# A hybrid encoder block on one core: the half's norm and gate as a second thread, joined key norms, four gate groups beside the mixers, turned values as a thread

## Chip, cores and metric

The kernel runs on one core of a Trainium2 chip. The metric is the device time of one execution in microseconds (us). A difference within 0.5% is treated as no change. The engines are named as in the profile: PE multiplies matrices, PEld loads its weights, DVE is the vector engine, ACT the scalar (activation) engine, POOL the general one, and SP issues most of the DMAs.

## What is computed

The input `x` is 256 positions of 2048 features. One layer is computed:

```python
u = RMSNorm(x)
proj = u @ w_in        # stick-breaking q,k,v | forgetting q,k,v,f | RWKV r,k,v + low-rank | three gates
y_A = stick_breaking_attention(...)    # 4 heads of 128
y_B = forgetting_attention(...)        # 4 heads of 128
y_C = rwkv7_time_mix(...)              # 16 heads of 64
m = sum_i sigmoid(gate_i) * (y_i @ P_i)
x = x + RMSNorm(m @ w_out)
x = x + RMSNorm(relu(RMSNorm(x) @ w_up)**2 @ w_down)
```

The RWKV mixer is a recurrence over positions. Its keys are normalised per head, and its output `y` goes through a group norm per head, a bonus term and a gate:

```python
kk = kk / max(sqrt(sum(kk*kk)), 1e-12)
state = state * w_t - (state @ kk_t) * kka_t + v_t * k_t ;  y_t = state @ r_t
y = (y - mean) * rsqrt(var + eps) * ln_w + ln_b + sum(r*k*r_k) * v ;  y_C = y * g
```

All values are float32. The large products split each factor into a rounded part (type fp32r) and a remainder, and add three of the four products of these parts.

## The kernel before

**Weights and the large products.** The weights lie in memory as one list of blocks of 128x1024 values (512 KB). `wraw` loads a block into one of three `raw` buffers through the SP queue. `wsplit` makes `whi` from it on ACT (line 140) and `wlo` on DVE (line 141); `wnext` keeps one block split ahead of the one in use. Three helpers use the blocks. `unit` makes 128 output features for all 256 positions from two blocks (`gemm`, lines 156, 160 and 164). `tok` makes 512 output features with positions on the partitions; a block of it is twelve PE instructions of 512 columns (lines 187 and 203).

**The order of the work on PE** is written by hand: from the start to the end of the branches PE runs its instructions in program order (`manual_schedule`, held open by `written`). The instructions of the other engines are ordered by a list scheduler: they may go as soon as what they read is there, and earlier program order has priority. So a PE instruction whose input is late holds all of PE, and the matmuls behind it too.

**The mixers are a generator.** `mixers()` emits stick-breaking attention (`sb_mix`), forgetting attention (`fox_mix`), the low-rank parts (`rwkv_lora`) and then the two halves of the RWKV heads (`rwkv_half(0)`, `rwkv_half(1)`), a few instructions at a time. It yields either a number, the us that have to pass before its next piece, or a key, the name of a value that it needs. The products call `tick` after each few matmuls. `tick` moves a clock of the program forward by `US` = 0.227 us for each matmul it counts and calls `step`, which emits the mixers' next pieces if their time has come. A key counts as there `SETTLE` = 2.6 us after it was marked. This clock knows only the matmuls of the large products, and it is a matter of emission order: nothing on the chip waits for it.

**A half** (`rwkv_half`, four groups of two heads) goes through these stages: key norms in two pairs (lines 522 to 548, with Ln and Exp on ACT); for each group the scores, decays and bonus (552 to 615); a transposed copy of the values (617 to 627); the inverse of 32 triangular blocks in 31 steps on DVE (635 to 645) and two small products that complete it (655 to 669, PE lines 657 and 664); a loop over four chunks of 64 positions that carries the state (678 to 726, PE lines 683, 687, 696, 706, 710 and 714); and the group norm, bonus and gate in two pairs (737 to 763, PE lines 746, 759 and 760; `rsqrt` has Ln and Exp on lines 227 and 228). The small PSUM results of the mixers share four buffers (`mps`), the large products have four others (`gps`).

**After the projections** the kernel runs four groups of gate and branch for y_A and y_B, then two groups of gate for y_C (`thc`, line 867), with the mixers between them. What the mixers have left then is emitted at once by the loop of lines 868 to 870, with no product between. After it come the split of y_C into `ycp`, two branches for y_C, the two last gates, the two last branches, and between these the transposed values of m (`turn`, line 878), which w_out needs as `mpk`.

Of the kernel before, what the change touches and what calls it, by code (L numbers as in the profile page):

```python
# [17 lines left out]
T = 256  # L18
# [32 lines left out]
def hybrid_block(ctx, tc, xt, x, gains, params, consts, lora, gup, wst, out):  # L51
# [43 lines left out]
    mix = [None]  # L95
    wait = [None]
    fin = [False]
    clock, due = [0.0], [0.0]

    def step():  # L100

        if mix[0] is None or fin[0]:
            return False
        if wait[0] is not None:
            if wait[0] not in at or clock[0] < at[wait[0]] + SETTLE:
                return False
            wait[0] = None
        try:
            r = next(mix[0])
        except StopIteration:  # L110
            fin[0] = True
            return False
        if isinstance(r, str):
            wait[0] = r
        else:
            due[0] = clock[0] + r
        return True

    def tick(us):

        clock[0] += us
        while clock[0] >= due[0] and step():
            pass

# [27 lines left out]
    def gemm(ps, hi, lo, pks, first, last, tick=lambda us: None):  # L152

        n = len(pks)
        for i in range(n - 1 if last else n):
            PE.matmul(ps, hi[:, i * 128:i * 128 + 128], pks[i], start=first and i == 0, stop=False)  # L156
            if i % 3 == 2:
                tick(3 * US)
        for i in range(n):
            PE.matmul(ps[:, 0:T], lo[:, i * 128:i * 128 + 128], pks[i][:, 0:T], start=False, stop=False)  # L160
            if i == 3:
                tick(4 * US)
        if last:
            PE.matmul(ps, hi[:, (n - 1) * 128:n * 128], pks[n - 1], start=False, stop=True)  # L164
        tick(4 * US)
# [241 lines left out]
    def fox_mix():  # L407
# [17 lines left out]
        yield 10.0  # L425
# [15 lines left out]
        for h in range(4):  # L441
            ps = mps()
            PE.matmul(ps[:, 0:128], q[h][:, 0:128], k[h][:, 0:128], start=True, stop=True)
            PE.matmul(ps[:, 128:384], q[h][:, 128:256], k[h], start=True, stop=True)
            V.scalar_tensor_tensor(w[:, h, 0:128], ps[:, 0:128], ATT_SCALE, cb[:, h, 0:128], ALU.mult, ALU.subtract)
            V.scalar_tensor_tensor(w[:, h, 128:384], ps[:, 128:384], ATT_SCALE, cb[:, h, :], ALU.mult, ALU.subtract)
            V.scalar_tensor_tensor(w[:, h, 0:128], w[:, h, 0:128], ct[:, h:h + 1], C("madd"), ALU.add, ALU.add)
            V.tensor_scalar(w[:, h, 128:256], w[:, h, 128:256], ct[:, 4 + h:5 + h], None, ALU.add)
            V.scalar_tensor_tensor(w[:, h, 256:384], w[:, h, 256:384], ct[:, 4 + h:5 + h], C("madd"),
                                   ALU.add, ALU.add)  # L450
            if h % 2:
                yield 6.0
# [54 lines left out]
    def rwkv_half(hf):  # L507
# [13 lines left out]
        lora_load(PR[0])  # L521
        for i2 in range(2):
            ss = []
            for p in PR[2 * i2:2 * i2 + 2]:
                yield f"k{p}"
                kx[p] = done[f"k{p}"]
                s = tmp()
                A.activation(s, kx[p], AF.Square, scale=P("kk", p))
                ss.append(s)
            yield 2.4  # L530
            ps = mps()
            for i in range(2):
                PE.matmul(ps[:, i * T:i * T + T], C("bones"), ss[i], start=True, stop=True)

            ri = B6[:, 2 * i2:2 * i2 + 2, :]
            sc = B6[:, 4:6, :]
            sq = rp.tile([128, 2, T], F32, tag="At", name=nm("sq"), bufs=2)
            V.tensor_scalar(sq, ps.rearrange("p (a b) -> p a b", a=2), 1e-24, None, ALU.max)
            A.activation(sc, sq, AF.Ln, scale=float(2.0 ** 20))
            A.activation(ri, sc, AF.Exp, scale=-0.5)  # L540
            yield 2.5
# [3 lines left out]
            V.tensor_tensor(sc, sc, sq, ALU.mult)  # L545
# [71 lines left out]
        XT = []  # L617
        for i2 in range(2):
# [59 lines left out]
        for c in range(4):  # L678
# [13 lines left out]
            yield 2.6  # L692
# [8 lines left out]
            yield 2.8  # L701
# [24 lines left out]
            yield 3.4  # L726

        gqs = {}
# [8 lines left out]
        gup_load(PR[0])  # L737
        for i2 in range(2):
            B6 = rp.tile([128, 6, T], F32, tag="b6", name=nm("gn"), bufs=1)
            var, ri, sc = B6[:, 0:2, :], B6[:, 2:4, :], B6[:, 4:6, :]  # L740
            for i in range(2):
                A.activation(sc[:, i, :], y[PR[2 * i2 + i]], AF.Square)
            yield 2.4
            ps = mps()
            for i in range(2):
                PE.matmul(ps[:, i * T:i * T + T], C("bones"), sc[:, i, :], start=True, stop=True)
            A.activation(var, ps.rearrange("p (a b) -> p a b", a=2), AF.Identity, scale=1.0 / 64, bias=cst[:, 1:2])
            yield 1.5
            rsqrt(ri, var, sc)
            yield 6.0  # L750
            for i in range(2):
                p = PR[2 * i2 + i]
                V.tensor_tensor(y[p], y[p], ri[:, i, :], ALU.mult)
                A.activation(y[p], y[p], AF.Identity, scale=P("lnw", p), bias=P("lnb", p))
                V.tensor_tensor(y[p], y[p], bon[p], ALU.add)
                gup_load(p + 1)
                gq = gqs[p]
                ps = mps()
                PE.matmul(ps[:, 0:T], gq[:, 0, :], sy, start=True, stop=False)
                PE.matmul(ps[:, 0:T], gq[:, 1, :], sz, start=False, stop=True)  # L760
                V.tensor_tensor(y[p], ps[:, 0:T], y[p], ALU.mult)
                yc[p] = y[p]
                yield 2.5
# [8 lines left out]
    mix[0] = mixers()  # L772
# [10 lines left out]
    def mark(key, value=True):  # L783
        done[key], at[key] = value, clock[0]

    g0 = 16 + 8 + 6 + 16 + 8 + 48
    order.extend(range(wpos[0], g0))
# [3 lines left out]
    for g in (0, 2):  # L791
        for i in (0, 8):
            order.extend(c0 + 12 * (g + j) + k for j in range(2) for k in (range(8) if i == 0 else range(8, 12)))

    for br in ("sb", "fox"):
        for s in ("q", "k"):
            if br == "sb":
                continue
            lst = []
            for h in range(4):  # L800
                ps = unit(upk)
                t = g1()
                evac(ps, t)
                lst.append(t)
            done[br + s] = lst
        done[br + "v"] = vtok()
        mark(br)
        if br == "sb":
            for i, (nme, n) in enumerate((("zx", 128), ("zy", 128), ("zz", 36))):
                ps = unit(upk)  # L810
                z = rp.tile([128, T], F32, name=nme)
                if n < 128:
                    G.memset(z, 0.0)
                shift(ps, MU_X + i, z[0:n], n)
                done[nme] = z
            mark("lora")
# [11 lines left out]
    while "yb" not in done:  # L828
        assert step() or not fin[0]
    ya, yb = done["ya"], done["yb"]  # L830

    def gate(spare=False):
        ths = []
        for ps in tok(upk):
            if spare:
                th = [g1(), g1()]
            else:
                t = rp.tile([128, 512], F32, tag="th", name=nm("th"), bufs=3)
                th = [t[:, 0:T], t[:, T:]]
            if spare:  # L840
                for i in range(2):
                    A.activation(th[i], ps[:, i * T:i * T + T], AF.Tanh, scale=0.5)
            else:
                A.activation(t, ps, AF.Tanh, scale=0.5)
                th = [t]
# [3 lines left out]
    def branch(ys, ths, m, first):  # L849

        for tt, ps in enumerate(tok(ys)):
            n = 512 // len(ths[tt])
            for i, th in enumerate(ths[tt]):
                cs = slice(i * n, i * n + n)
                if first:
                    V.scalar_tensor_tensor(m[:, tt, cs], th, 1.0, ps[:, cs], ALU.add, ALU.mult)
                else:
                    V.scalar_tensor_tensor(th, th, 1.0, ps[:, cs], ALU.add, ALU.mult)
                    V.tensor_tensor(m[:, tt, cs], m[:, tt, cs], th, ALU.add)

    ms = []
    for g in range(4):
        m = rp.tile([128, 2, 512], F32, tag="m", name=nm("m"), bufs=4)
        branch(ya, gate(), m, True)
        branch(yb, gate(), m, False)
        ms.append(m)
    thc = [gate(), gate(True)]
    while not fin[0]:
        due[0] = clock[0]
        step()  # L870
# [5 lines left out]
    mpk = []  # L876

    def turn(g):

        for j in range(4):  # L880
            ps = mps()
            for tt in range(2):
                PE.transpose(ps[:, tt * 128:tt * 128 + 128], ms[g][:, tt, j * 128:j * 128 + 128], C("ident"))
            u = pk()
            split(ps[:, 0:T], u, 0.5)
            mpk.append(u)

    branch(ycp, thc[0], ms[0], False)
    branch(ycp, thc[1], ms[1], False)
    thc = [gate(), gate(True)]  # L890
    turn(0)
    branch(ycp, thc[0], ms[2], False)
    turn(1)
    branch(ycp, thc[1], ms[3], False)
    turn(2)
    turn(3)
    written.close()
# [43 lines left out]
    for g in range(4):  # L941
        gs = slice(512 * g, 512 * g + 512)
        for tt, ps in enumerate(tok(mpk, 4 if g == 3 else 1)):
# [419 lines left out]
```

## Time and profile before

| | |
|---|---|
| median of three runs | 1579.47 us (1574.84 to 1582.13) |
| the profiled execution, its own time | 1581.91 us |
| its span from first to last instruction | 1580.1 us |
| mean granted PE clock | 0.982 of full speed |
| weights and other input read | 279.77 MB |
| part looked at here | from the start to about 860 us: projections, mixers, gates, branches, w_out |

In the profile a row of the timeline gives the start, the length, the engine, the line of the kernel, the operation and its operands, and, in brackets, the idle time of the engine before it and what released it. A row of the table by stages gives, for each stretch, its length and for each engine the busy time and the number of instructions, then the granted PE clock, the share of time in which the DMA engines were busy, and their GB/s. A matmul of the mixers (plain fp32) is two PE instructions in the trace: the 32 of line 657 are 64.

### The profile page before, as it was taken

The numbers are of one execution on the slowest core, as the hardware profiler recorded it, in microseconds if no ns is written. First come the engines' busy times: TensorE is split into PE (matmuls) and PEld (weight loads), VectorE is DVE, ScalarE is ACT, GpSimd is POOL, SyncE is SP. The second block draws the span as 40 slices with busy tenths as digits, with TensorE's granted clock in tenths as the row PEclk, the third lists the DMA queues.
The fourth block names the chain that finished last, engine by engine and source line by source line (L and its number), as shares of the span: only waits on it lengthen the run. The fifth ranks groups of instructions, "written<-read, shape, count | busy, mean of one in ns | idle before, by whom it ended". The sixth has DMA issues, their size and how long they took to land.

```text
span 1580.1 us, 22365 instructions
## 1 busy us (share of the span) xinstructions
PE 1530.9 (97%) x8318; PEld 1279.6 (81%) x8318; DVE 1160.4 (73%) x1566; ACT 901.7 (57%) x1340; POOL 85.8 (5%) x155
## 2 busy tenths in 40 slices
PE   7999999999999999779999999999999999999997
PEld 6888888888788788668888788887888887888885
DVE  6875567797457789255654867888988899888855
ACT  7564467554457553254444766666765676666542
POOL 0020001100000100000000000000000000000000
PEclk9999999999999999689999999999999999999999
DMA  7645555456445545126595466878888887888764
GB/s 260 190 154 182 168 166 172 150 169 201 142 144 172 165 158 173 55 71 192 178 329 202 151 189 180 248 230 260 249 258 235 231 264 227 266 239 239 211 203 135
DMA packets 101053, 308.50 MB, mean 195 GB/s; under 512 B 10064, under 2 KB 12496, under 8 KB 100816
## 3 DMA queue, kind: packets, MB, share of 16 engines
q1 hardware_dynamic: 90624, 278.56, 53.4%
q0 software_dynamic: 6912, 25.17, 8.6%
q10 hardware_dynamic: 3408, 3.34, 0.6%
q8 instruction: 65, 1.06, 0.3%
q14 instruction: 44, 0.36, 0.1%
HBM read 279.77 MB, written 2.10 MB: 178 GB/s over the span
## 4 chain that ended last, share of the span: by engine, by line
PE 72%; issue 11%; DMA 9%; DVE 5%; ACT 2%; POOL 0%; ACTq 0%; POOLq 0%; DVEq 0%; SPq 0%
PE gps L203 29%; PE gps L156 15%; PE gps L160 8%; PE gps L187 6%; DMA raw<-raw 5%; DMA raw<-in_wst_dram 4%; DVE wlo L141 2%; ACT whi L140 1%; PE gps L164 1%; PE mps L1128 1%; PE mps L1130 1%; PE mps L1129 1%; PE gps L1130 1%; PE gps L1128 1%; PE gps L1129 1%
## 5 line engine op out<-in xcount | busy, mean ns | idle before, releaser
L141 DVE TENSOR_TENSOR wlo<-raw,whi 128x1024 fp32r<-128x1024 f32 x590 | 717.0, 1224 | 259.7 <-ACT whi L140 236.5
L140 ACT ACTIVATE whi<-raw 128x1024 fp32r<-128x1024 f32 x590 | 618.5, 1055 | 352.2 <-PE gps L203 130.5
L156 PE MATMUL gps<-pk,whi 128*128 128x512 f32 x1495 | 382.8, 394 | 1.1 <-DVE tmp L1051 1.0
L156 PEld LDWEIGHTS gps<-pk,whi 128*128 128x128 f32 x1495 | 277.3, 189 | 59.4 <-issue 5.1
L203 PE MATMUL gps<-whi,pk 128*128 128x512 f32 x1144 | 288.8, 392 | 0.0
L203 PEld LDWEIGHTS gps<-whi,pk 128*128 128x128 f32 x1144 | 213.9, 188 | 44.9 <-issue 0.5
L160 PEld LDWEIGHTS gps<-pk,wlo 128*128 128x128 f32 x1599 | 218.6, 190 | 16.0 <-issue 0.6
L160 PE MATMUL gps<-pk,wlo 128*128 128x256 f32 x1599 | 224.6, 282 | 0.0
L203 PE MATMUL gps<-wlo,pk 128*128 128x512 f32 x572 | 155.7, 392 | 0.0
L203 PEld LDWEIGHTS gps<-wlo,pk 128*128 128x128 f32 x572 | 106.9, 188 | 23.1 <-issue 0.7
L1128 PE MATMUL mps<-whi,fm 128*128 128x512 f32 x192 | 76.3, 397 | 0.8 <-ACT whi L140 0.7
L1130 PE MATMUL mps<-wlo,fm 128*128 128x512 f32 x192 | 75.8, 395 | 0.8 <-DVE wlo L141 0.8
L1050 ACT ACTIVATE tmp<-gps 128x256 f32<-128x256 f32 x64 | 24.6, 384 | 89.1 <-PE gps L164 88.8
L1129 PE MATMUL mps<-whi,fm 128*128 128x512 f32 x192 | 75.1, 391 | 0.0
L187 PE MATMUL gps<-whi,pk 128*128 128x512 f32 x264 | 71.8, 393 | 0.9 <-DVE pk L220 0.8
L1095 POOL DMA_DIRECT2D raw<-raw x48 | 41.9, 873 | 555.3 <-DVE raw L1092 360.0
L1130 PE MATMUL gps<-wlo,fm 128*128 128x512 f32 x144 | 57.6, 400 | 2.2 <-DVE wlo L141 1.7
L1092 DVE TENSOR_TENSOR raw<-raw,raw 128x1024 f32<-128x1024 f32 x48 | 58.7, 1223 | 1.0
L187 PEld LDWEIGHTS gps<-whi,pk 128*128 128x128 f32 x264 | 49.3, 188 | 12.2 <-DVE pk L220 1.2
L1128 PE MATMUL gps<-whi,fm 128*128 128x512 f32 x144 | 56.9, 395 | 1.5 <-ACT whi L140 1.4
L1129 PE MATMUL gps<-whi,fm 128*128 128x512 f32 x144 | 56.4, 392 | 0.0
L203 PE MATMUL gps<-whi,fm 128*128 128x512 f32 x208 | 51.4, 389 | 0.0
(309 smaller groups left out, 1580.3 us busy)
## 6 DMA issues: line engine op xcount, KB each, us to landing
raw<-in_wst_dram SPq DMA_DIRECT2D x518, 512.0 KB, 4.4
raw<-raw POOLq DMA_DIRECT2D x48, 512.0 KB, 6.5
x<-in_x_dram SPq DMA_DIRECT2D x8, 256.0 KB, 5.3
out_dram<-x SPq DMA_DIRECT2D x8, 256.0 KB, 2.8
x<-in_xt_dram ACTq DMA_DIRECT2D x1, 1024.0 KB, 9.7
fm<-in_gains_dram SPq DMA_DIRECT2D x4, 256.0 KB, 4.3
pk<-in_gains_dram SPq DMA_DIRECT2D x4, 256.0 KB, 4.7
con<-in_consts_dram SPq DMA_DIRECT2D x1, 576.0 KB, 9.2
```

The lines of the kernel that those rows point to most:

```text
L140: A.activation(hi, raw, AF.Copy)
L141: V.tensor_tensor(lo, raw, hi.bitcast(F32), ALU.subtract)
L156: PE.matmul(ps, hi[:, i * 128:i * 128 + 128], pks[i], start=first and i == 0, stop=False)
L160: PE.matmul(ps[:, 0:T], lo[:, i * 128:i * 128 + 128], pks[i][:, 0:T], start=False, stop=False)
L187: PE.matmul(ps[tt], pks[k][:, c:c + 128], w[:, (k - k0) * 512:(k - k0) * 512 + 512], start=k == 0 and part == 0 and w is hl[0], stop=w is ...
L203: PE.matmul(ps[tt], pks[k][:, c:c + 128], w[:, (k - k0) * 512:(k - k0) * 512 + 512], start=k == 0 and part == 0 and w is hl[0], stop=False)
L1050: A.activation(b, ps[0][:, T:2 * T], AF.Copy)
L1092: V.tensor_tensor(R[a], R[a], R[b], ALU.add)
L1095: G.dma_start(out=R[a], in_=R[b], accum_op=ALU.add)
L1128: PE.matmul(Q[f], a, w, start=d == 0 and i == 0, stop=False)
L1129: PE.matmul(Q[f], b, w, start=False, stop=False)
L1130: PE.matmul(Q[f], a, wl, start=False, stop=d == 3 and i == 1)
```

## The change

- **Threads.** The one generator becomes a list `threads`. `start` adds one, `step` advances one of them, `tick` advances all whose time has come, and `finish` runs the clock on without products until all threads (or one key) are done.
- **Norm and gate.** The end of `rwkv_half` (group norm, bonus, gate) becomes `gate_norm`, which a half starts as a thread when its chunk loop is done. It does all four groups at once in buffers of other tags (`XT`, `Ti`), marks `gn0` or `gn1` at its end, and the second half waits for `gn0` ahead of its stage of transposed values.
- **Key norms** of a half are made for all four groups together: four squares, two products, then two Ln and two Exp side by side.
- **Gates.** All four gate groups of y_C come ahead of the end of the mixers (`thc` has four), the third and fourth in buffers of the tag `BK`. Then `finish()`, the split, and four branches in a row.
- **Turned values.** `turn` becomes a thread `turns()` that makes each group's transposes 2.6 us after its branch is marked; the last group's m goes to two `pk` buffers. PE's hand-written order now ends ahead of the last group of w_out.
- **Clock and waits.** `gemm` counts 22 matmuls for a unit where it counted 28, at finer steps. The yields of the chunk loop go from 2.6, 2.8 and 3.4 to 2.0, 2.2 and 2.6, those of `fox_mix` from 10 and 6 to 9 and 5.
- **Order of the projections.** The third low-rank unit comes right after the stick-breaking values, the other two after the forgetting values.

```diff
-        while clock[0] >= due[0] and step():
+        while any([step(th) for th in list(threads)]):
             pass
+    def finish(key=None):
+        while threads if key is None else key not in done:
+            clock[0] += US
+            tick(0.0)
...
-            if i % 3 == 2:
-                tick(3 * US)
+            if i % 2:
+                tick(2 * US)
...
-            if i == 3:
-                tick(4 * US)
+            if i % 4 == 3:
+                tick(2 * US)
...
-        tick(4 * US)
...
+        for i, p in enumerate(PR):
+            yield f"k{p}"
+            kx[p] = done[f"k{p}"]
+            A.activation(rin[i], kx[p], AF.Square, scale=P("kk", p))
+        yield 2.6
...
+        for i2 in range(2):
+            A.activation(B6[:, 2 * i2:2 * i2 + 2, :], sq[i2], AF.Ln, scale=float(2.0 ** 20))
+        for i2 in range(2):
+            A.activation(ri, ri, AF.Exp, scale=-0.5)
+        yield 4.5
...
+        if hf:
+            yield "gn0"
...
-            yield 2.6
+            yield 2.0
...
-            yield 2.8
+            yield 2.2
...
-            yield 3.4
+            yield 2.6
+        start(gate_norm(hf, y, bon, sy, sz))
...
+    def gate_norm(hf, y, bon, sy, sz):
+        gup_load(PR[0])
+        var = rp.tile([128, 4, T], F32, tag="XT", name=nm("gn"), bufs=2)
+        ri = rp.tile([128, 4, T], F32, tag="XT", name=nm("gn"), bufs=2)
+        sc = rp.tile([128, 4, T], F32, tag="Ti", name=nm("gn"), bufs=1)
+        for i, p in enumerate(PR):
+            A.activation(sc[:, i, :], y[p], AF.Square)
+            if i % 2:
+                yield 1.6
         for i2 in range(2):
+            ps = mps()
+            for i in range(2):
+                PE.matmul(ps[:, i * T:i * T + T], C("bones"), sc[:, 2 * i2 + i, :], start=True, stop=True)
+            A.activation(var[:, 2 * i2:2 * i2 + 2], ps.rearrange("p (a b) -> p a b", a=2), AF.Identity, scale=1.0 / 64,
+                         bias=cst[:, 1:2])
+        yield 2.0
+        rsqrt(ri, var, sc)
+        yield 7.5
+        for i, p in enumerate(PR):
...
+            yield 2.0
+        mark(f"gn{hf}")
...
-    thc = [gate(), gate(True)]
-    while not fin[0]:
-        due[0] = clock[0]
-        step()
+    thc = [gate(), gate("g1"), gate("BK"), gate("BK")]
+    finish()
...
+    start(turns())
+    for g in range(4):
+        if g < 3:
+            branch(ycp, thc[g], ms[g], False)
+        else:
+            m = [pk().bitcast(F32) for _ in range(2)]
+            branch(ycp, thc[g], ms[g], False, m)
+            ms[g] = m
+        mark(f"m{g}")
```

214 lines of the change are left out of this document (95 added, 119 removed).

## The prediction

> **What bounds the kernel now.** I read the page first, then the stages of the first half, then PE's waits, then PE's timeline at the one place that stands out.
>
> ```profile
> PE   7999999999999999779999999999999999999997
> PEclk9999999999999999689999999999999999999999
> ```
>
> In 40 slices of 39.5 us PE is busy in nearly all of nearly every one; apart from start and end, PE and its clock drop only in the slices from about 630 to 710 us. The table by stages shows that place; its columns are length, then busy time of PE, PEld, DVE, ACT and POOL, granted clock, DMA share and GB/s.
>
> ```profile
> 640.00:660.00 20.00, 15.44 (x186) 13.40 (x186) 5.24 (x14) 3.95 (x17) 0.00 (x0) 0.59 0.01 2
> 660.00:680.00 20.00, 16.64 (x124) 14.22 (x123) 3.01 (x9) 5.54 (x17) 0.20 (x1) 0.51 0.00 0
> 680.00:700.00 20.00, 13.54 (x51) 10.38 (x49) 12.26 (x24) 13.07 (x20) 0.20 (x1) 0.83 0.09 26
> ```
>
> No weights move (2 and 0 GB/s), and the clock granted is 0.59 and 0.51. PE's timeline says why: from 633.47 on there is no large product, only the second half's end, from line 657 to the last gate product (line 760).
>
> ```profile
> 632.92 0.61 PE L187 MATMUL gps<-wlo,pk 128*128 128x512 f32 x2
> 633.47 0.75 PE L657 MATMUL mps<-TW,SC 32*32 32x32 f32 x64
> ...
> 675.25 2.07 PE L746 MATMUL mps<-gn,con 128*128 128x256 f32 x4 [0.96 <-ACT gn L742]
> ...
> 690.46 0.59 PE L760 MATMUL mps<-zz,gup 128*128 128x256 f32 x2
> 690.70 2.20 PE L203 MATMUL gps<-whi,pk 128*128 128x512 f32 x8
> ```
>
> PE's waits (total, times, longest) are few over the whole execution, and past the start most lie in or right behind this stretch:
>
> ```profile
> PE mps L746 <- ACT gn L742: 7.2, 2, 6.2
> PE mps L683 <- DVE PB L721: 3.0, 2, 1.5
> PE mps L696 <- ACT rh L690: 2.6, 4, 1.0
> PE gps L187 <- DVE pk L220: 0.8, 1, 0.8
> ```
>
> So in the first 860 us PE is the bound, and what a change can take away is the stretch without products, less the mixers' own PE work in it.
>
> **Term 1, the uncovered stretch.** It lasts 690.70 - 633.47 = 57.23 us. What would its PE work cost beside products? The first half does the same steps there. I count the large products between its line 657 and its line 746, for line 203 in the first row and line 187 in the second (stage, length, busy PE and in brackets its instructions), and take the rate of these from three rows of the timeline.
>
> ```profile
> 387.55:453.85 66.30, 43.56 (x175) 31.74 (x174) 1.00 0.46 146
> 387.55:453.85 66.30, 8.98 (x36) 6.69 (x36) 1.00 0.46 146
> ```
>
> ```profile
> 610.50 1.98 PE L203 MATMUL gps<-whi,pk 128*128 128x512 f32 x8
> 612.31 1.07 PE L203 MATMUL gps<-wlo,pk 128*128 128x512 f32 x4
> 613.22 1.98 PE L203 MATMUL gps<-whi,pk 128*128 128x512 f32 x8
> ```
>
> Twelve products take 613.22 - 610.50 = 2.72 us, 0.2267 each. The 211 take 47.8 of the 66.30 us; the other 18.5 are lines 657 to 714, at clock 1.00 and without a wait. For the group norm:
>
> ```profile
> 453.85 1.02 PE L746 MATMUL mps<-gn,con 128*128 128x256 f32 x4
> 454.52 1.28 PE L203 MATMUL gps<-whi,pk 128*128 128x512 f32 x4
> 455.64 1.08 PE L203 MATMUL gps<-wlo,pk 128*128 128x512 f32 x4
> ```
>
> ```profile
> 481.09 0.59 PE L759 MATMUL mps<-zy,gup 128*128 128x256 f32 x2
> 481.52 0.59 PE L760 MATMUL mps<-zz,gup 128*128 128x256 f32 x2
> 481.77 1.28 PE L187 MATMUL gps<-whi,pk 128*128 128x512 f32 x4
> 482.89 0.62 PE L187 MATMUL gps<-wlo,pk 128*128 128x512 f32 x2
> ```
>
> A pair's line 746 with four products takes 455.64 - 453.85 = 1.79 us, 0.91 of it the products: 0.88. Lines 759 and 760 with four take 1.80: 0.89. Two and four of these are 5.3 us. Covered, the stretch costs 18.5 + 5.3 = 23.8; the gain is **57.2 - 23.8 = 33.4 us**. The clock is in this sum: the covered rows ran at 1.00.
>
> **Is it covered to its end?** That depends on the emission clock alone, and the code fixes it. I went through ticks and yields in order, from the mark of the forgetting values on (clock 0 there). Products: 26 units of 22 counts, four groups of 2 x 96 + 2 x 24 counts and four gates of 96, in all 1916 x 0.227 = 435.0 us. Mixers: 2.6 settle, 46.5 forgetting attention, 3 low-rank; each half 17.1 key norms, 56 for the four groups, 8 + 40.4 (31 steps: 18.6 + 0.004 x 5456) + 10.5 + 6.4 for the inverse, 27.2 chunks, 165.6 in all; 20.7 for the last gate norm. That is 404.0, and about 160 yields are each rounded up to the next tick, which adds 29.6: the last thread ends at 433.6, **1.4 us before the last gate**. No yield waits for a projection after the forgetting values; `gn0` is marked long before it is asked for. Before, the same count has the mixers at line 657 as the gates end, which is what the trace shows.
>
> **Term 2, the join behind it.** The row for line 220 above, 0.8 us, is `ycp` arriving late. After the change the seven earlier groups are done while the last gate runs; I take 0.8 gained; at worst the last group comes as late again and it is 0. The four `BK` buffers of the late gates come from `Bt` and `Kt`, last read in the fourth chunk, emitted 3 us before the first is needed: 0.
>
> **Term 3, the middle, where half 0's gate norm and half 1's key norms now run side by side.** Before they ran one after the other (last three stages; the first row is the second half's inverse, for comparison):
>
> ```profile
> 600.00:620.00 20.00, 20.00 (x90) 16.56 (x89) 19.21 (x39) 7.68 (x9) 0.00 (x0) 1.00 0.57 191
> ...
> 460.00:480.00 20.00, 20.00 (x90) 16.56 (x89) 13.82 (x21) 13.78 (x17) 0.42 (x2) 1.00 0.52 166
> 480.00:500.00 20.00, 20.00 (x90) 16.56 (x89) 14.97 (x21) 12.99 (x17) 0.41 (x2) 1.00 0.60 193
> 500.00:520.00 20.00, 20.00 (x90) 16.08 (x89) 16.47 (x25) 13.90 (x19) 1.76 (x4) 1.00 0.50 162
> L141 DVE TENSOR_TENSOR wlo<-raw,whi 128x1024 fp32r<-128x1024 f32 x590 | 717.0, 1224 | 259.7 <-ACT whi L140 236.5
> L140 ACT ACTIVATE whi<-raw 128x1024 fp32r<-128x1024 f32 x590 | 618.5, 1055 | 352.2 <-PE gps L203 130.5
> ```
>
> A block each 2.72 us takes DVE 1.22 (45%) and ACT 1.06 (39%), so 9.0 and 7.8 of each 20 us. The mixers' share of these 60 us is then about 45.3 - 27 = 18 us of DVE and 40.7 - 23.4 = 17 us of ACT. Now it has 22 us of clock, with the mixers' PE work (5.3 and the key norms') about 28 us real, in which the blocks take 12.6 and 10.9: 31 and 28 us of work for 28. Both engines are full. Late data holds PE: gate products hold `mps` buffers until line 761 has read them, half 1's scores (line 600) need all four, and every product queues behind them. I take **-4 us**: 3 that DVE lacks and 1 for the chain's latency. The bounds are 0 (squares and loads depend on nothing late and run ahead) and -15: if ACT and DVE strictly take turns, the mixers' 18 + 17 = 35 us stand in one chain, and at some 20 steps of it half a `wlo` or `whi` (0.6 and 0.5) is in the way on average at two steps of three, 8 more, 43 for 28.
>
> One more thing can weigh on such a wait, the clock. In the stretch it was 0.59 from 640 to 660 us though no single wait there passed 1.5 us (line 683). The Trainium skill, "TensorE: Matmul & The Clock Gate", Part 1, has it at half speed after an idle window of about 3.4 us and until one such window was busy. By that rule one wait of 4 us would cost up to 1.7 us more, an estimate from that page, and the time would be 1553.5; it would also leave the stretch from 640 to 660 at full clock, which the trace contradicts. The sum doesn't use it, and the 1.7 us lie inside the forecast's own spread.
>
> Joining also saves four Ln/Exp pairs. ACT stands beside PE here, so it counts at nothing; if the cover is gone, it is a part of the -4.
>
> ```profile
> 495.38 1.28 ACT L540 ACT_TABLE_LOAD   x1
> 496.67 0.63 ACT L540 ACTIVATE b<-b 128x512 f32<-128x512 f32 x1
> ```
>
> Each pair has two table loads of 1.28, so 8 fewer are 10.3 us of ACT. The Trainium skill, "ScalarE: Activation LUTs", What ACT_TABLE_LOAD costs, prices a switch at 1.28 plus a drain of 1.38; by that it would be 21.3 us of ACT, and still 0 of the time. The trace shows no such drain: the activation starts 1.29 us after its load did.
>
> **Term 4, shorter yields in the chunk loop.** How near was it to a wait? In the first half's first chunk DVE hands over the second copy (line 700) just ahead of line 706:
>
> ```profile
> 403.81 0.28 DVE L700 COPY XT<-mps 64x128 f32<-64x128 f32 x1
> 404.20 0.69 PE L706 MATMUL mps<-XT,Kt 128*64 128x64 f32 x16
> ```
>
> 0.11 us to spare, with 2.8 us of yield; 2.2 makes it about 0.5 late. I assume that four of the eight chunks are so near, so **-2 us**. Bounds: 0, and -7, if each of the 24 waits loses 0.3.
>
> **Term 5, the rest.** In the units the clock counts 22 for 24 real (28 before), so the mixers' yields last longer there: 0, cover unchanged. The turned values move 2.6 us behind their branch; DVE needs two steps of 512 columns (about 0.6 each, by half the 1.22 of line 141) and perhaps a `wlo` (1.22), 2.4 in all: 0 to -2, I take -0.5. The reordered low-rank units and the later end of PE's hand order move the same instructions, and no queue is longer for them; SP's loads of the next stage follow the last branch as they did: 0. `gup` loads (two per group on ACT's queue) are the same.
>
> **Sum**, against the profiled execution (1581.9 us; its span 1580.1, the median 1579.5, 0.15% lower): 33.4 + 0.8 - 4 - 2 - 0.5 = 27.7 us, 1554.2. From the median, by the same difference: **1551.8**.
>
> **Rivals.**
> *No new wait at all*: the other engines run ahead, as they do before (DVE was at 19.2 of 20 us in the inverse, and PE at 20.00). The gain is 34.2: 1545.3. Chance 0.17.
> *The middle is overloaded*: PE waits there for a chain through ACT and DVE that is longer than its room. For it: both engines at or over 100%. Against it: only 3 us over. With -15 for -4 the time is 1562.8. Chance 0.16; of that 0.03 for one so long (over 26 us) that the change is within 0.5%.
> *The change doesn't do what it says*: the cover ends before the gate norm does. For it: 1.4 us of spare in 435. Then its stretch stays bare, from 675.25 - 0.96 to 690.70, less 5.3 of PE work, 11.1 us: 1562.9. Chance 0.05.
> *Slower*: the shortened yields starve all 24 waits of the chunk loops. Bare, they cost up to 1.0 (line 696) and 1.5 (line 683) in the list above, and a `whi` and a `wlo` ahead of each add 2.3. If PE waits 1.9 us at each, about half of that, 45.6 us go in place of term 4's 2, and the time is 1595.4; it decides at 1.2 us each (27.7 + 2 over 24). Against it: the first half's loop ran with yields 0.6 to 0.8 longer and not one wait. Chance 0.04.
>
> **How the numbers follow.** The forecast has 0.58. 0.5% is 7.9 us, about what a measurement of this kernel can tell from no change. Faster: 0.58 + 0.17 + 0.13 + 0.05 = 0.93; same 0.03; slower 0.04. The range 1543 to 1563 holds the forecast, no new wait, and the two cases near 1562.8 in their better half; about 0.16 is outside.
>
> **What would show it.** Right: line 657 of the second half between rows of line 203, DMA near 190 GB/s and clock 1.00 throughout 380 to 860 us, w_out some 28 us earlier, waits of 4 us among lines 600, 746, 759, 203 near half 0's gate norm, under 3 us in lines 683 to 714. Wrong: a stretch without line 203 before `ycp`, waits over 10 us in the middle, or a drop of the clock there.

## The result, and the profile after

The changed kernel takes 1552.39 us (median of four runs, 1549.91 to 1554.30), the kernel before 1577.48 us on the same chip: a ratio of 0.9837, 95% interval 0.9807 to 0.9867. A second comparison on another occasion gave 0.9833 (0.9808 to 0.9858). The forecast was 1551.8 us. The profiled execution took 1552.68 us, its span 1550.9; both are 29.2 us shorter than before. A gain of 27.7 us was forecast; the medians show 25.1 (the interval of the ratio allows 21 to 30), so that the forecast time is off by only 0.6 us is in part chance.

Of the page, the busy share of PE and its granted clock in 40 slices of the span:

```profile
PE   7999999999999999999999999999999999999997
...
PEclk9999999999999999999999999999999999999999
```

The dip that stood at 630 to 710 us is gone. The table by stages, with the columns of before (length; busy time and instructions of PE, PEld, DVE, ACT, POOL; clock; DMA share; GB/s):

```profile
480.00:500.00 20.00, 18.01 (x84) 14.51 (x85) 16.20 (x28) 11.11 (x18) 2.60 (x9) 0.91 0.53 174
640.00:660.00 20.00, 20.00 (x193) 15.73 (x192) 9.15 (x13) 8.30 (x18) 0.00 (x0) 1.00 0.32 111
660.00:680.00 20.00, 19.69 (x170) 15.69 (x169) 8.09 (x14) 8.91 (x22) 0.00 (x0) 1.00 0.31 106
680.00:700.00 20.00, 20.00 (x91) 16.70 (x89) 13.91 (x18) 15.05 (x19) 0.41 (x2) 1.00 0.51 169
```

From 640 to 700 us PE is busy for 59.69 of 60 us at full clock. The stage that got worse most is 480 to 500: it was full before, and now PE lacks 2.0 us there and the clock is 0.91. Three others that were full (from 360, 400 and 440 us on) lack 0.3 to 0.5 us each, by the smaller waits below. PE's timeline shows the second half's end between products now (old line 657 is line 671, 664 is 678, 203 is 213; the chunk loop's 683 to 714 are 697 to 728, the group norm's 746 is 765, the gate's 759, 760 and 761 are 778, 779 and 780, and 187 is 197):

```profile
621.88 1.07 PE L213 MATMUL gps<-whi,pk 128*128 128x512 f32 x4
622.88 0.75 PE L671 MATMUL mps<-TW,SC 32*32 32x32 f32 x64
623.57 1.20 PE L213 MATMUL gps<-whi,pk 128*128 128x512 f32 x4
```

PE's waits (total, times, longest), four of those in the part that was changed (a fifth, 0.3 us at line 171, was there before with 0.2):

```profile
PE mps L778 <- DVE g L780: 2.0, 1, 2.0
...
PE mps L724 <- DVE XT L714: 0.7, 2, 0.3
PE gps L197 <- DVE wlo L152: 0.5, 1, 0.5
...
PE mps L720 <- DVE XT L714: 0.3, 1, 0.3
```

Nothing waits for `ycp`, and nothing at line 902, the turned values. The largest new one is a wait of 2.0 us of a gate product (line 778).

For the accounts below I use one landmark: the start of the first transposition of x behind w_out. All that is edited in the change and in the experiments lies ahead of it. It is the first row of line 966 in the kernel before,

```profile
870.83 1.23 PE L966 MATMUL mps<-ident,x 128*128 128x128 f32 x8 [0.29 <-DVE x L937]
```

and of line 987 in the changed kernel:

```profile
841.59 1.29 PE L987 MATMUL mps<-ident,x 128*128 128x128 f32 x8 [0.27 <-DVE x L955]
```

It comes 29.2 us earlier, and what is behind it takes 709.3 us in both. So the whole gain was made ahead of the landmark.

### The profile page after: what moved, and what is told of

Same layout as the page of the kernel before. It is cut to its first block, busy times and chain, and to the rows that moved or that the text cites. A ratio compares the mean times of both kernels' runs of the same rounds, so it can differ in the third digit from the quotient of the medians.

```text
span 1550.9 us, 22351 instructions
## 1 busy us (share of the span) xinstructions
PE 1515.4 (98%) x8318; PEld 1263.7 (81%) x8318; DVE 1157.1 (75%) x1554; ACT 891.9 (58%) x1326; POOL 84.0 (5%) x155
## 4 chain that ended last, share of the span: by engine, by line
PE 28%; issue 12%; DMA 11%; DVE 4%; ACT 1%; POOL 0%; POOLq 0%; DVEq 0%; SPq 0%; ACTq 0%
PE gps L213 12%; DMA raw<-raw 7%; PE gps L167 6%; DMA raw<-in_wst_dram 5%; PE gps L171 3%; PE gps L197 3%; DVE wlo L152 2%; ACT whi L151 1%; PE mps L1149 1%; PE mps L1151 1%; PE mps L1150 1%; PE gps L1151 0%; PE gps L175 0%; PE gps L1149 0%; PE gps L1150 0%
```

## The experiments

Two questions were open. Which part of the change brings the gain? And what holds PE in the middle: that DVE and ACT are full there, as the prediction had it, or something else? The table gives every run in the order of the sections below. Ratios are to the kernel before on the same chip, measured beside each group of kernels (its medians were 1577.5 to 1582.2 us); landmark and span are of the profiled execution, and "rest" is their difference.

| kernel | median us | ratio to before (95%) | landmark | span | rest |
|---|---|---|---|---|---|
| before | 1577.48 | 1 | 870.8 | 1580.1 | 709.3 |
| the change | 1552.39 | 0.9837 (0.9807 to 0.9867) | 841.6 | 1550.9 | 709.3 |
| a0_after, the change again | 1554.47 | 0.9833 (0.9808 to 0.9858) | 841.5 | 1549.3 | 707.8 |
| e2_gates_only | 1564.31 | 0.9899 (0.9884 to 0.9914) | 859.1 | 1561.9 | 702.8 |
| e1_two_gates | 1571.50 | 0.9935 (0.9913 to 0.9958) | 864.4 | 1574.4 | 710.0 |
| e3_inline_norm | 1557.54 | 0.9848 (0.9826 to 0.9869) | 848.7 | 1557.2 | 708.5 |
| e4_late_gate | 1551.16 | 0.9813 (0.9799 to 0.9828) | 842.6 | 1550.3 | 707.7 |
| e6_gate_weights | 1552.61 | 0.9823 (0.9798 to 0.9848) | 844.3 | 1549.9 | 705.6 |
| e7_gate_weights_late | 1547.58 | 0.9791 (0.9765 to 0.9817) | 839.5 | 1544.2 | 704.7 |
| e8_pair_norms | 1544.45 | 0.9769 (0.9749 to 0.9789) | 836.4 | 1541.5 | 705.1 |
| e12_joined_later | 1549.82 | 0.9785 (0.9766 to 0.9804) | 838.2 | 1548.5 | 710.3 |
| e5_old_clock | 1550.13 | 0.9798 (0.9773 to 0.9823) | 842.4 | 1550.6 | 708.2 |
| e11_turns_inline | 1553.86 | 0.9832 (0.9812 to 0.9851) | 846.0 | 1552.5 | 706.6 |
| e9_best | 1549.39 | 0.9816 (0.9789 to 0.9842) | 841.1 | 1547.1 | 706.0 |

The rest, which no experiment edits, varies from 702.8 to 710.3 us from one profiled execution to another. A difference of a few us between two medians is therefore weak evidence, and the landmark the better measure of an edit: two executions of the change have it at 841.6 and 841.5 us. It has a scatter of its own all the same. In e3, e5 and e9, and in no other, the clock drops near 177 us with no wait of PE (last section), and 1.7 us of their landmarks is that drop. The expectation for the run of the change itself:

> The changed kernel itself, as the measure for the three beside it. 0.981 to 0.987 of the kernel before; waits of PE as in its first profile: 2.0 us at line 778 for line 780, 1.0 at lines 720 and 724.

It repeated the change, with the same 2.0 us at line 778.

### Which part brings the gain

**e2_gates_only** is the kernel before with four gates ahead of the mixers' end, and nothing else.

```diff
-    thc = [gate(), gate(True)]
+    thc = [gate(), gate(True), gate(False, "BK"), gate(False, "BK")]
...
-    thc = [gate(), gate(True)]
     turn(0)
-    branch(ycp, thc[0], ms[2], False)
+    branch(ycp, thc[2], ms[2], False)
```

> The kernel before with four gates of y_C ahead of the end of the mixers, nothing else changed. Theory: the emission clock has the mixers in the third chunk of the second half when the gates end; the rest, about 31 us bare with 11.5 us of PE work, is lost, so of 33.4 us only 14 are gained: 1561 to 1566 us. Rival (more gates are all that matters): 1545 to 1552.

The median is in the expected range. A stage and two rows of PE (line numbers of the kernel before):

```profile
700.00:720.00 20.00, 12.47 (x56) 9.74 (x57) 6.60 (x15) 9.06 (x20) 0.41 (x2) 0.59 0.03 8
```

```profile
718.13 2.07 PE L746 MATMUL mps<-gn,con 128*128 128x256 f32 x4 [5.78 <-ACT gn L742]
...
722.79 2.20 PE L203 MATMUL gps<-whi,pk 128*128 128x512 f32 x8
```

The two gates cover a part of what was bare. From line 696 of the third chunk (689.42) on there is no product until 722.79, 33.4 us where about 31 were expected, and the group norm stands in it at clock 0.59. By the landmark the gates alone bring 11.7 us of the 29.2.

**e1_two_gates** is the opposite: the change, but with the third and fourth gate behind the second branch, where they were.

```diff
-    thc = [gate(), gate("g1"), gate("BK"), gate("BK")]
+    thc = [gate(), gate("g1")]
...
-    start(turns())
     for g in range(4):
+        if g == 2:
+            thc += [gate(), gate("g1")]
+            start(turns())
```

> The changed kernel with two gates of y_C ahead of the end of the mixers instead of four (the other two stand between the branches, as before). Theory (the cover of the late second half made the gain): the gates end after the first of four chunks, so three chunks and the last gate norm stand bare: 29.9 us of chunks less 13.4 of PE work, and about 16.5 of norm less 5.3, 27.7 us lost. 1577 to 1583 us, about the time of before, with a stretch of some 45 us without large products. Rival (the threads, joined norms and shorter yields made the gain themselves): 1555 to 1565.

It came out between the two: 0.9935, with the landmark 6.5 us earlier than before. The stage shows the bare stretch again, and PE's rows its end:

```profile
660.00:680.00 20.00, 14.50 (x93) 11.63 (x92) 2.70 (x7) 8.40 (x21) 0.41 (x2) 0.62 0.02 5
```

```profile
671.71 3.75 PE L765 MATMUL mps<-gn,con 128*128 128x256 f32 x8 [0.96 <-ACT gn L759]
...
681.90 2.20 PE L213 MATMUL gps<-whi,pk 128*128 128x512 f32 x8
```

The theory had the bare stretch too long: 46.4 us, where it is 36.1 (from 645.82, within the second chunk, to 681.90). The chunks stand bare for 24.9 us instead of 29.9, since the gates cover a part of the second one too, and the norm for 11.1 instead of 16.5. Done for four groups at once it is over 10.2 us after it began on PE (671.71 to 681.90), where two pairs, one behind the other, took 15.5 with a wait of 6.2 between them.

Gates alone bring 11.7 us and the rest of the change alone 6.5, together 18.2; both at once bring 29.2. The remaining 11 us need both: the cover is long enough only if the mixers also end sooner.

**e3_inline_norm** keeps everything but the second thread: half 1 starts after half 0's norm and gate.

```diff
-        start(gate_norm(hf, y, bon, sy, sz))
+        yield from gate_norm(hf, y, bon, sy, sz)
```

> The changed kernel with the gate norm of each half emitted in line, not as a thread. Theory: by the emission clock the last gate norm begins as the gates end and stands bare, 11 us lost, while the wait and the clock drop in the middle (2.0 and 1.7 us) go: 1557 to 1563 us. Rival (the thread only shifts work): 1551 to 1553.

0.9848, at the near edge of what the theory expected, and the landmark 7.2 us later than in a0. The wait in the middle is gone, and PE is full there, but the mixers outlast the last gate:

```profile
698.96 1.89 PE L765 MATMUL mps<-gn,con 128*128 128x256 f32 x8
...
704.84 0.67 PE L778 MATMUL mps<-zy,gup 128*128 128x256 f32 x2 [2.26 <-DMA gup<-in_gup_dram]
...
707.62 3.36 PE L213 MATMUL gps<-whi,pk 128*128 128x512 f32 x8
...
725.81 0.98 PE L902 MATMUL mps<-ident,m 128*128 128x128 f32 x7 [2.02 <-DVE m L877]
```

8.7 us without a product, and eight products behind it that take 3.2 us instead of 1.8. Then comes a wait that a0 doesn't have, of 2.0 us at line 902, with the clock low behind it again; why it comes isn't shown. Of the 7.2 us, 1.7 are the clock drop near 177 us, far ahead of what was edited. Even so the thread is worth its wait: the 3.6 us that it costs in the middle are more than won back at the end.

### What holds PE in the middle

The timeline of the changed kernel around the wait, PE and one row of DVE:

```profile
473.26 0.59 PE L778 MATMUL mps<-zy,gup 128*128 128x256 f32 x2
...
476.44 0.59 PE L778 MATMUL mps<-zy,gup 128*128 128x256 f32 x2
...
479.25 0.48 PE L566 MATMUL mps<-zx,lor 64*128 64x256 f32 x1
479.26 0.48 PE L568 MATMUL mps<-zx,lor 64*128 64x256 f32 x1
...
481.91 0.41 DVE L780 TENSOR_TENSOR g<-mps,g 128x256 f32<-128x256 f32 x1
...
482.37 1.22 PE L778 MATMUL mps<-zy,gup 128*128 128x256 f32 x2 [1.99 <-DVE g L780]
```

Four `mps` buffers are there. The first two gate products hold two of them, and half 1's decays (lines 566 and 568) take the other two. The third gate product needs the buffer of the first, which line 780 reads only at 481.91. After the wait the clock is low; single microseconds:

```profile
482.00:483.00 1.00, 0.63 (x2) 0.54 (x3) 1.00 (x3) 0.98 (x3) 0.00 (x0) 0.68 0.64 152
483.00:484.00 1.00, 1.00 (x5) 0.82 (x3) 1.00 (x2) 1.00 (x3) 0.00 (x0) 0.50 0.95 369
484.00:485.00 1.00, 1.00 (x4) 0.82 (x3) 1.00 (x4) 0.74 (x3) 0.20 (x1) 0.50 0.24 53
485.00:486.00 1.00, 1.00 (x4) 0.77 (x4) 1.00 (x2) 0.58 (x2) 0.00 (x0) 0.61 0.94 315
```

Busy time times what the clock lacks: 0.2 + 0.5 + 0.5 + 0.4 = 1.6 us. The wait and its clock cost 3.6 us together. Why is line 780 late? DVE is busy in every one of these microseconds, and in those of the wait itself, so "DVE is full" is a theory; that the decays take the buffers at the wrong moment is another.

**e4_late_gate** has half 0's gate emitted 5.5 us later, so that what line 780 reads is ready.

```diff
-        yield 7.5
+        yield 7.5 if hf else 13.0
```

> The changed kernel with 13.0 instead of 7.5 us ahead of the first half's gate products. Theory (gate products take the four small PSUM buffers too early, PE waits 2.0 us for line 780 and its clock then drops, 1.7 us): both go, 1548 to 1550 us, no wait at line 778 and clock 1.00 from 480 to 500. Rival (ACT and DVE are full in the middle whatever the order): the wait moves to the scores of the second half, 1551.5 to 1553.

```profile
487.48 0.67 PE L778 MATMUL mps<-zy,gup 128*128 128x256 f32 x2 [1.31 <-DMA gup<-in_gup_dram]
489.26 0.67 PE L779 MATMUL mps<-zz,gup 128*128 128x256 f32 x2 [1.10 <-DMA gup<-in_gup_dram]
```

The wait for line 780 is gone, and two for the gate's weights stand in its place: they have only two buffers, and their DMA is issued late. The landmark is 1.1 us later than in a0, and the median lies between the two ranges.

**e6_gate_weights** loads the gate's weights of a half at once into buffers that are free by then (the second product has 32 rows instead of 128 of which 96 are zero).

```diff
-                gqs[p] = gq = rp.tile([128, 2, 128], F32, tag="gup", name=nm("gup"), bufs=2)
+        gq = rp.tile([128, 4, 128], F32, tag="PB", name=nm("gup"), bufs=1)
+        gz = rp.tile([64, 4, 128], F32, tag="rh", name=nm("guz"), bufs=1)
+        nc.scalar.dma_start(out=gq.rearrange("p a b -> p (a b)"), in_=gup[0:128, cols])
+        nc.scalar.dma_start(out=gz[0:32].rearrange("p a b -> p (a b)"), in_=gup[128:160, cols])
```

> The changed kernel with the gate's weights of a half loaded at once into two buffers that are free after the chunk loop, instead of group by group through two buffers. Theory (the wait in the middle is for a PSUM buffer that line 780 has not yet read; the weights' DMA is the next wait behind it, as the later gate products showed): the wait of about 2 us for line 780 and the clock drop stay, the time is within 2 us of the changed kernel. Rival (the DMA of the weights was the cause all along): 3 to 4 us less.

The wait for the buffer stays, as the theory had it (line 771 is the gate product here):

```profile
481.85 0.70 PE L771 MATMUL mps<-zy,gup 128*128 128x256 f32 x2 [1.39 <-DVE g L773]
```

It is shorter, 1.4 us, but the clock behind it was 0.50 for twice as long, which costs 3.4 us instead of 1.6; the first and the last whole microsecond at that clock:

```profile
483.00:484.00 1.00, 1.00 (x3) 0.45 (x2) 1.00 (x4) 0.71 (x2) 0.00 (x0) 0.50 0.44 176
...
488.00:489.00 1.00, 1.00 (x3) 0.46 (x2) 0.00 (x0) 1.00 (x2) 0.33 (x1) 0.50 0.39 139
```

The edit also does something that it was not meant to: the product with 32 rows is dearer on PE. A gate group with four large products takes 2.18 us (478.88 to 481.06 in e7), where with 128 rows it takes 1.80 (473.45 to 475.25 in e12). That is 0.38 more for each of the eight groups, and it is in the landmarks of e6, e7 and e9.

**e7_gate_weights_late** does both edits, e6 and the 13.0 of e4.

> The same with 13.0 instead of 7.5 us ahead of the first half's gate products. Theory (both limits, PSUM buffers and weights, are gone): no wait of PE over 0.5 us in the middle, clock 1.00 from 460 to 520 us, 3 to 4 us less than the changed kernel. Rival (ACT and DVE are full): the wait moves to the scores of the second half (lines 612 to 618) and the time stays within 1.5 us.

```profile
480.00:500.00 20.00, 20.00 (x97) 14.55 (x96) 18.48 (x33) 11.77 (x19) 2.29 (x5) 1.00 0.57 188
```

No wait and full clock, though DVE does more in these 20 us (18.48) than in the changed kernel (16.20). The median is 0.9791, the landmark 2.0 us earlier than in a0: the 3.6 of the wait and its clock and 0.7 of small waits are gone, and about half of that goes into 2.2 us more of work on PE, where the dearer products are. All four gate products now stand between the first decays and the second.

**e8_pair_norms** makes the key norms in two pairs again and keeps the rest of the change. The prediction had counted their joining at nothing.

```diff
-        for i, p in enumerate(PR):
-            yield f"k{p}"
-            kx[p] = done[f"k{p}"]
-            A.activation(rin[i], kx[p], AF.Square, scale=P("kk", p))
-        yield 2.6
         for i2 in range(2):
+            for p in PR[2 * i2:2 * i2 + 2]:
+                yield f"k{p}"
+                kx[p] = done[f"k{p}"]
+                A.activation(s, kx[p], AF.Square, scale=P("kk", p))
+            yield 2.4
...
-        yield 4.5
+            yield 2.5
```

> The changed kernel with the key norms of a half in two pairs, as before. Theory (the join matters only by its shorter emission, 2.7 us of yields a half; the ACT table loads it saves are hidden): by the emission clock the last 4 us of the last gate norm stand bare, which costs 0 to 2 us, since its products wait for nothing that is late; elsewhere the middle has a little more room. Same as the changed kernel to 2 us more. Rival (the saved table loads shortened the path): 3 to 6 us more, with longer PE waits in the middle.

Both theories missed: it is the fastest kernel of all, 0.9769 (0.9749 to 0.9789), an interval wholly below that of the change, and its landmark is 5.0 us earlier. PE in the middle (lines 776 and 564 are the gate product and the decays here):

```profile
483.45 0.59 PE L776 MATMUL mps<-zy,gup 128*128 128x256 f32 x2
...
485.83 0.48 PE L564 MATMUL mps<-zx,lor 64*128 64x256 f32 x1
```

```profile
480.00:500.00 20.00, 20.00 (x103) 15.79 (x101) 18.71 (x34) 12.13 (x19) 3.70 (x9) 1.00 0.49 155
```

The fourth gate product now stands ahead of the decays, and PE is full from 480 to 500 us at clock 1.00. The pairs take longer by the emission clock, so half 1's decays are emitted later. Is it this delay that helps, or the order of the norms on ACT and DVE?

**e12_joined_later** tells these apart: joined norms, and only the delay.

```diff
-            yield 3.0
+            yield 3.0 if hf == 0 or i2 == 0 else 7.0
```

> The changed kernel with one number different: after the joined key norms of half 1 the emission waits 7.0 us instead of 3.0, so that half 1's decays and everything of half 1 behind them come 4 us later by the emission clock, as they do with the key norms in pairs, while the norms themselves stay joined. Theory (the pairs were faster because the decays of half 1 came later and no longer took the mps buffers between the gate products): the wait for the gate (2.0 us) and the half clock behind it go, the windows from 480 to 500 us show TensorE at 20.00 and clock 1.00, and the time is near that of the pairs, 1542-1550 us where before is about 1581. Rival (it is the joining itself, by the order in which the norms stand on ScalarE and VectorE): the wait stays or moves to another line between 460 and 500 us, and the time stays at 1551-1556 us.

0.9785 (0.9766 to 0.9804), in the range of the theory. Its timeline beside that of the changed kernel:

```profile
479.58 0.59 PE L778 MATMUL mps<-zy,gup 128*128 128x256 f32 x2
...
482.10 0.42 DVE L780 TENSOR_TENSOR g<-mps,g 128x256 f32<-128x256 f32 x1
...
482.52 0.59 PE L778 MATMUL mps<-zy,gup 128*128 128x256 f32 x2
...
485.32 0.48 PE L566 MATMUL mps<-zx,lor 64*128 64x256 f32 x1
```

```profile
480.00:500.00 20.00, 20.00 (x103) 15.98 (x102) 19.30 (x33) 12.37 (x19) 4.62 (x9) 1.00 0.65 201
```

Line 780 runs at 482.10, no earlier than the 481.91 of the changed kernel: DVE is just as late. But the third gate product started at 479.58, because the decays had not yet taken the other two buffers, and PE is full at clock 1.00. Nor has DVE less to do: over the 28 us from 465 to 493 it is busy for 25.71 here and for 25.99 in the changed kernel, where PE has 28.00 and 26.01. So the cause is the order in which the two threads take the buffers. The landmark is 3.2 us earlier than in a0, of the 3.6 that the wait and its clock cost. Small waits of the chunk loop and for `wlo` (1.4 us in all, against 0.7 in e8) are a part of the 1.8 us by which e8's landmark is still ahead; the remainder of that, and the 5 us between their rests, stay open. The intervals of the two ratios overlap.

### The small terms

**e5_old_clock** undoes the finer clock of `unit` (28 counts again) and the shorter yields of the chunk loop.

```diff
-            if i % 2:
-                tick(2 * US)
+            if i % 3 == 2:
+                tick(3 * US)
...
+        tick(4 * US)
...
-            yield 2.0
+            yield 2.6
```

> The changed kernel with the old count of ticks in the units (28) and the old yields of the chunk loop (2.6, 2.8, 3.4). By the emission clock the mixers then end 9.5 us before the last gate instead of 1.4, so nothing is bare. Theory (the short yields cost about 1 us of waits at lines 720 and 724, and nothing else hangs on them): those waits go, 0.5 to 2 us less than the changed kernel. Rival (the new clock avoided waits of the attention mixers beside the units): new waits before 270 us, same time or more.

The waits in the chunk loop are gone, and so is the one of 2.0 us at line 778: the new emission order moves the middle too. Two of PE's waits are new:

```profile
PE gps L198 <- DVE wlo L152: 2.0, 1, 2.0
...
PE mps L569 <- DVE g L781: 0.7, 1, 0.7
```

The first ends at 360.8 us, with clock 0.91 from 360 to 380, and the landmark is 0.9 us later than in a0. Of that, 1.7 are the clock drop near 177 us, so without it the landmark would be 0.8 us earlier. What the chunk loop and the middle gain is nearly given back by one wait for `wlo` and its clock. The theory was right on the chunk loop and wrong that nothing else hangs on the emission clock; the rival's waits before 270 us did not come.

**e11_turns_inline** makes the turned values in line again, one branch late, as a function instead of a thread.

```diff
-    start(turns())
     for g in range(4):
...
-        mark(f"m{g}")
+        if g:
+            turn(g - 1)
+    turn(3)
```

> The changed kernel with the turned values emitted in line, one branch later, the last group right behind the last branch. Theory (the thread hides only the wait for the last m): PE waits 1.5 to 2.5 us for DVE at the last transposes and nothing else changes, 1.5 to 3 us more than the changed kernel. Rival (the transposes were hidden anyway): within 0.5 us.

```profile
PE mps L900 <- DVE pk L233: 2.0, 1, 2.0
```

The wait stands at 740 to 760 us, the clock there is 0.91 (1.7 us lost), and the landmark 4.5 us later than in a0; the median did not show it (0.9832). So the thread spares a wait that the prediction had not counted.

**e9_best** joins e7 and e5.

> The gate's weights at once, 13.0 us ahead of the first half's gate products, and the old count of ticks and chunk yields. Theory (each wait has its own cause): the middle and the chunk loops are free of waits, but the wait of 2.0 us for wlo behind the first inverse that the old clock brought stays, with its clock drop; 0 to 4 us above the version with the weights and the 13.0 alone. Rival (the wait for wlo came from the crowded middle): it goes and the time is 1 to 3 us below that version.

0.9816 (0.9789 to 0.9842): no better than e7, in the range of the theory, and a wait of 1.3 us for `wlo` is back, as in e5. The landmark is 1.7 us later than in e7, as much as the clock drop near 177 us cost. Pairs with the gate weights of e6 were not tried.

## Why the prediction was right, and where a step failed

**The uncovered stretch** (term 1) and **the join** (term 2) were right in mechanism and size. The account at the landmark: 33.4 and 0.8 as forecast, and 0.8 for a wait of line 187 for `wlo` (at 631 us, just ahead of the old stretch) that the sum had left out, make 35.0. From it go 3.6 in the middle, 1.0 in the chunk loop and 0.5 for `wlo` at line 197: 29.9, where 29.2 were measured, so 0.7 us have no name. A count that doesn't use these terms agrees. Added up over rows of 1 us from 20 us to the landmark, PE's idle time fell from 19.7 to 4.0 us and what the clock lacked while PE was busy from 16.9 to 1.6, while the rest, PE's own work, grew by 1.8. In the old stretch (633 to 691 us) it was 17.5 idle and 16.9 of clock: half of what the missing products cost was the clock.

**The cover** did reach the end, as the emission clock said: no wait for `ycp`. Experiment e3 shows how little there was to spare, e1 that without the gates it isn't there.

**The middle** (term 3) was forecast at -4 and cost 3.6, but the step to it failed. "Both engines are full" did not hold PE. The working had 31 us of DVE and 28 of ACT for 28 us; over 465 to 493 us DVE had 25.99 and ACT 18.03. Over 480 to 500 us DVE had 16.20 and ACT 11.11 of 20, and in e7, e8 and e12 DVE did more in the same time with PE at 20.00. The prediction named the `mps` buffers, but as victims of late data, and expected half 1's scores to wait; in fact half 1's decays took two buffers between the second and the third gate product, and the gate waited (old line 759, one of the four lines that the prediction listed). One number of the emission order (e12) removes it. That the size fitted was chance: the 4 us were to be waits alone, and the sum left the clock out; 2.0 of wait and 1.6 of clock came.

**Joined key norms** "count at nothing" was right for the saved table loads: e8 has four more of them (two joined halves have 4 at these lines, the pairs 8; 5.1 us of ACT) and is the faster kernel. It was wrong for the kernel: the joined norms end sooner by the emission clock, which moved half 1's decays in between the gate products. What the step left out is the time at which the pieces behind a shortened one are emitted.

**The chunk loop** (term 4) cost 1.0, not 2.0: three waits of about 0.3 of 24. **Turned values** (term 5) cost nothing.

Of what was to be seen, the products beside line 671 and w_out 29.2 us earlier were there, and the clock was full from 630 to 710 us. It was not full throughout: 0.91 from 480 to 500 us is a drop in the middle, which the prediction had named as a sign of being wrong, and there the account of term 3 was wrong. DMA near 190 GB/s was not there either: 106 to 111 from 640 to 680 us, where PE shares the time with the mixers' own matmuls (170 to 193 instructions of PE in 20 us instead of 90) and so asks for fewer weights.

**Rivals.** *Overloaded middle*, *cover ends too soon* and *slower* did not come. *No new wait* is what e8 shows: the landmark 34.4 us earlier than before, the 34.2 of that rival.

## What to carry to other kernels

The worth of a cover is the bare stretch less its own work at the covered rate, and it holds only if the covered work also ends in time; parts that bring 11.7 and 6.5 us alone can bring 29.2 together. Where two threads share a few PSUM buffers on an engine that runs in program order, count for each moment who holds a buffer until which read: a shift of emission by 4 us, from an edit elsewhere, can cost more than that edit saves. Measure an edit at a landmark behind it, keep the scatter of the untouched rest (7.5 us here) out of the verdict, and look ahead of the edit for clock drops that it can't have caused (1.7 us each here).

## What was not expected of the hardware

Short waits can halve the clock, or not. In the changed kernel 2.0 us of waiting brought 0.50 to 0.68 for about 3.4 us, in e6 1.4 us of waiting about twice that. And a wait of the same length at the same place behaves in both ways. Line 987 of the changed kernel waits 1.81 us; its row of PE and the microseconds behind it:

```profile
844.70 1.62 PE L987 MATMUL mps<-ident,x 128*128 128x128 f32 x8 [1.81 <-DVE x L955]
```

```profile
845.00:846.00 1.00, 1.00 (x7) 0.52 (x6) 1.00 (x4) 0.83 (x2) 0.00 (x0) 1.00 0.00 0
846.00:847.00 1.00, 1.00 (x4) 0.38 (x4) 1.00 (x3) 1.00 (x5) 0.00 (x0) 1.00 0.00 0
```

In e8 the same line (985 there) waits 1.82 us:

```profile
839.54 1.90 PE L985 MATMUL mps<-ident,x 128*128 128x128 f32 x8 [1.82 <-DVE x L953]
```

```profile
840.00:841.00 1.00, 1.00 (x5) 0.69 (x6) 1.00 (x4) 0.98 (x3) 0.00 (x0) 0.69 0.00 0
841.00:842.00 1.00, 1.00 (x5) 0.54 (x3) 1.00 (x3) 1.00 (x6) 0.00 (x0) 0.50 0.00 0
```

Full clock in the one, half in the other. The clock can also drop with no wait at all. At 174 to 178 us the changed kernel and e3 run the same instructions, in this order and within 0.1 us of the same times, small matmuls of the forgetting attention and then large products, with PE busy throughout. The row from 178 us in the changed kernel and in e3:

```profile
178.00:179.00 1.00, 1.00 (x6) 0.83 (x5) 0.90 (x1) 0.00 (x0) 0.00 (x0) 1.00 0.00 0
```

```profile
178.00:179.00 1.00, 1.00 (x4) 0.71 (x4) 0.88 (x1) 0.00 (x0) 0.00 (x0) 0.50 0.00 0
```

What sets it off is not shown. Each of these short drops costs 1.5 to 1.7 us, the one in e6 3.4. The Trainium skill, "TensorE: Matmul & The Clock Gate", Part 1, has the activity judged in free-running windows of 3413 ns; the lengths of one and about two such windows, and that the same wait may or may not count, agree with it. Its condition, a whole idle window, does not: 1.4 us without a matmul were enough in e6. In these runs a wait of 1.3 to 2.0 us cost its own length and, of clock, nothing (1.3 us in e9, line 987 in the changed kernel), 1.5 to 1.7 us, or 3.4 (e6).
